# A state-space recurrence in blocks of four steps, inside a five-layer model on one core

## Chip, cores and metric

The kernel runs on one core of a Trainium2 chip. The metric is device microseconds of that core for one execution; every time below is in us unless ns is said.

## What is computed

The model is one hybrid layer, then four others. Only the first layer's state-space branch is touched here. In the reference, `u` has 512 tokens and 512 channels, in 32 groups of 16; each group has 64 complex states:

```python
lb_re = mag * jnp.cos(a_im * dt); lb_im = mag * jnp.sin(a_im * dt)     # lambda, per group and state
bu = einsum('blgc,gpc->blgp', u, bb)                                   # complex input, bb = B (lambda-1)/a
x[t] = lambda * x[t-1] + bu[t]                                         # associative scan over 512 tokens
y = einsum('gcp,blgp->blgc', c_re, x_re) - einsum('gcp,blgp->blgc', c_im, x_im) + d * u
out = gelu(y) * sigmoid(gelu(y) @ w_glu + b_glu)
```

Beside it the same layer has eight attention heads with a difference of two softmaxes, whose q, k and v come from `w_in`, and gates, from `w_in` too.

## The kernel before

Features lie on partitions and the 512 tokens along the free dimension. Dense products are done in three one-pass matmuls on split operands (fp32r, `mm3` and `tok`: lines 251 to 255 and 290 to 292); everything else on TensorE is plain fp32, which each matmul of the program sends as two instructions. A tile framework puts the instructions of all engines in order from a timeline of its own, starting from program order; `weave` interleaves generators step by step in program order.

The recurrence works on 16 tiles of 128 states (two groups each); quarter q holds four tiles j and the 128 channels `u[q]`. A complex scan is made real by rotation: with C and S the cosine and sine of theta*t, the input is turned back by theta*t, scanned with the real factor |lambda| on each lane, and turned forward again. For one tile, `SSM.run` does:

- `tables` (lines 1028 to 1043): C and S for 512 tokens, doubled from 32 in four levels. Each level is two scalings on ScalarE (1040, 1041) and one sum on GpSimd (1042), for C and for S.
- line 1057: two matmuls of the block-diagonal `bb` (32 rows, 128 columns) with `u[q]`, 512 tokens each, into two banks.
- line 1060: four products with C and S from the banks on VectorE; 1061 and 1062: their sum and difference on GpSimd.
- line 1065: two scans over 512 tokens on VectorE.
- line 1067: four products, three on VectorE and one on GpSimd; 1068 and 1069: difference and sum on GpSimd.
- line 1071: two matmuls with the output matrices `cm` (128 rows, 32 columns) into 32 partitions of the bank `y`.

After four tiles line 1075 adds d*u and writes `u[q]` in place. `tab` and `work` have two sets, so that two tiles can be under way.

`first_block` weaves, for p = 0, 1, 2: the two attention heads of pair p (`diff_head`, 8 steps: scores L874 and mask L875, maximum L876, exponential L877, scaling L881, L882, transposes L885, product with v L889), 4, 6 and 6 steps of the recurrence (four steps for each quarter), the projections of pair p + 1 (`pair`: L290 to L292, rotation on VectorE L817, L826 and on GpSimd L823, transposes L833) and 6, 2, 2 of the 16 gate tiles. For p = 3 the two heads go beside `glu`, `sigmoids` and the last six gates. `glu` and `sigmoids` take their scratch from the ring `hf`, which the recurrence uses as well.

Of the kernel before, what the change touches and what calls it, by code (L numbers as in the profile page):

```python
# [16 lines left out]
P = 128  # L17
T = 512
# [21 lines left out]
# ---------------------------------------------------------------- constants of the shapes  # L40
def const_arrays():
# [11 lines left out]
    cols["half"] = ((p[:, None] // 16) % 2 == np.arange(P)[None, :] // 64)  # L53
# [22 lines left out]
class Ring:  # L76
    """tiles that are kept and taken in turn; a use ends, in program order, before the tile's turn comes again"""
# [10 lines left out]
class Kern:  # L88
# [56 lines left out]

    def masks(self):
        """0 and -1e30 above or below the diagonal, and the identity that adds them to a bank"""
# [109 lines left out]
    def wblock(self, w, kts, c0, ncol=256, tok=False, eng=None):  # L257
        """the K chunks of one group of columns: (first k, number of k, tiles)"""
# [6 lines left out]
    def feat(self, blk, j, xh, xl, parts=FULL):  # L265
        """one tile of 128 output features by 512 tokens: [(bank, first token, tokens)]"""
# [13 lines left out]
    def tok(self, blk, xh, xl):  # L280
        """256 output features, tokens on partitions: two banks of [128, 2, 256], one after the other"""
# [13 lines left out]
    def feat_steps(self, blk, j, xh, xl, use):  # L295
        """feat in steps of two k; use(bank) at the end"""
# [10 lines left out]
    def tok_steps(self, blk, xh, xl, use):  # L307
        """tok in steps of four k; use(half, bank) at the end of each half"""
# [28 lines left out]
    def stat(self, i, v, q, part):  # L337
        """sums of v and of its square; the last tile goes straight to the tensor engine"""
# [36 lines left out]
    def rsqrt2(self, v, out=None, log=False, o=0):  # L375
        """-2/sqrt(v): the table's value and one Newton step"""
# [13 lines left out]
    def ln_scale(self, o, w, X, pool=POOLK):  # L390
        """X <- -2 * (X - mean) * rstd, tokens o..; the differences fill the waits of the scale's chain"""
# [33 lines left out]
    def ln_apply(self, gx, bx, gh, bh, parts=HALF):  # L425
        """X <- LN(X)*gx+bx ; H <- LN(X)*gh+bh (columns; the gains carry -1/2)"""
# [31 lines left out]
    def rms_apply(self, g, parts=HALF, log=False):  # L458
        """H <- RMSnorm(X) * g (columns; the gain carries -1/2)"""
# [11 lines left out]
    # ---- feature-major x from and to DRAM  # L471
# [10 lines left out]
    def load_x(self, src, between=None):  # L482
        """x by halves of the tokens, with the mean squares; between: what to load between the halves"""
# [39 lines left out]
    def finish(self, dst, g, b):  # L523
        """the last norm with tokens on partitions: the function that takes 512 features of a tile of tokens"""
# [37 lines left out]
    # ---- adaLN: six vectors of 1024 as columns [128, 48]  # L562
# [11 lines left out]
    def adaln(self, w, brow):  # L574
        """steps of 512 of the 6144 outputs, then the dict of columns in self.mod"""
# [26 lines left out]
    def ln_cols(self, g, b, sc, sh):  # L602
        """columns of x (scaled by alpha for the coming residual) and of h = x*sc + sh"""
# [13 lines left out]
    def add_res(self, n, parts, gate):  # L617
        """X += gate * bank"""
# [8 lines left out]
    def feats(self, tiles, xh, xl, use, halves):  # L627
        """tiles: (block, index) each; use(i, part) takes the bank; by halves of the tokens, all tiles of the first first"""
# [4 lines left out]
    def down4(self, tiles, xh, xl, gate):  # L633
        """tiles 4 to 7 by halves of the tokens: the norm of the first half overlaps the second half"""
# [8 lines left out]
    def logexp(self, a, b):  # L643
        """the table set that has both exp and ln, loaded after a and b are there"""
# [5 lines left out]
    def table(self, func, dep):  # L650
        """have a function's table loaded before it is needed"""
# [96 lines left out]
    def proj_res(self, w, xh, xl, gate, mean=True, early=False):  # L748
        """X += gate * (w^T x), with the sums for the norm; early: the first tiles by halves too"""
# [16 lines left out]
def weave(*gens):  # L766
    """steps of several sequences in turn: (sequence, its number of steps)"""
# [33 lines left out]
def qk_heads(K, blk, tabs, name, out):  # L801
    """two heads of q or k: project, norm, rotate, transpose -> per head [128 = 2 x 64, tokens]"""
# [37 lines left out]
def lam_cols(K):  # L840
    """lambda and the columns [128, 2] it needs"""
# [15 lines left out]
def diff_head(K, q, k, v, nlam, gcol, inv, dst):  # L857
    """q, k: [2 x 64, tokens]; v: [128, 4, 128] by tokens"""
# [47 lines left out]
class SSM:  # L906
    """32 groups of 64 complex states and 16 channels; 16 tiles of 128 states (two groups)"""

    def __init__(self, K, are, aim):
# [14 lines left out]
        mag = self.mag = new("mag")  # L924
# [20 lines left out]
        tr = K.slot("trig")[:, 0:432].rearrange("p (a w i) -> p a w i", a=3, i=16)  # L945
        self.cw, self.sw, self.nsw = tr[:, 0], tr[:, 1], tr[:, 2]
# [4 lines left out]
        nc.gpsimd.tensor_scalar(out=self.nsw, in0=self.sw, scalar1=-1.0, scalar2=None, op0=ALU.mult)  # L951
        # (lambda - 1) / a
        nr, ni, den, x, cr, ci = (new(m) for m in ("nr", "ni", "den", "x", "cr", "ci"))
        tt(nr, mag, self.cw[:, 0, :], ALU.mult)
        nc.gpsimd.tensor_scalar(out=nr, in0=nr, scalar1=-1.0, scalar2=None, op0=ALU.add)
        tt(ni, mag, self.sw[:, 0, :], ALU.mult)
# [12 lines left out]
        # input matrices, block-diagonal, transposed: per four tiles [(j, g, c), 128 states], both parts  # L969
# [6 lines left out]
        self.bb = []  # L976
        tmp = small()[:, 0:256].rearrange("p (i c) -> p i c", c=16)
        for x0, x1, op in ((b[0], b[1], ALU.subtract), (b[1], b[0], ALU.add)):
            bd = small()
            nc.gpsimd.memset(bd, 0.0)  # L980
            bv = bd.rearrange("p (i g c) -> p i g c", g=2, c=16)
            r = small()[:, 0:256].rearrange("p (i c) -> p i c", c=16)
            tt(r, x0, bc(cr), ALU.mult)
            tt(tmp, x1, bc(ci), ALU.mult)
            for g in range(2):
                s = slice(64 * g, 64 * g + 64)
                tt(bv[s, :, g, :], r[s], tmp[s], op)
            ps = K.psa()
            for q in range(4):
# [1156 lines left out]
```

## Time and profile before

| what | value |
|---|---|
| median of three runs | 3927.3 (3927.06 to 3933.09) |
| profiled execution, span | 3925.7 |
| TensorE busy over the span | 3760.0 (96%) |
| VectorE, ScalarE, GpSimd busy | 2621.5, 2095.3, 1517.8 |
| stretch with the recurrence | 100 to 470 |
| in it: TensorE, VectorE, ScalarE, GpSimd busy | 341.0, 292.4, 205.7, 248.2 of 370 |
| in it: granted TensorE clock | 0.89 |

The profiled execution is one further execution of the same kernel, 1.6 below the median of the runs. Busy time of TensorE counts an instruction until its modelled end, at whatever clock was granted, so a busy engine at a clock below 1.00 does less work than the figure says. The clock has two levels, 1.2 and 2.4 GHz; 0.89 is a mean over a stretch.

### The profile page before, as it was taken

To read this page: it belongs to the slowest core of one execution; us is meant where nothing else is said; L and a number is where in the kernel's file an instruction comes from. 1 tells how busy PE (TensorE), PEld (TensorE's weight loads), DVE (VectorE), ACT (ScalarE), POOL (GpSimd) and SP (SyncE) were. 2 spreads that over 40 slices of the span, in tenths; PEclk is the share of its full clock that TensorE was granted. 3 is DMA by queue.
4 is the path that set the end of the run, shared out by engine and by line. 5 is a ranking of instruction groups with operands and counts; after the bars stand their busy time and mean duration, and the time that the engine had idled before them with its cause. 6 is when DMAs were issued, how large, how long until landed. Compare 5 with 4: busy or idle time off the path is not lost.

```text
span 3925.7 us, 51300 instructions
## 1 busy us (share of the span) xinstructions
PE 3760.0 (96%) x19014; PEld 3058.9 (78%) x19014; DVE 2621.5 (67%) x3881; ACT 2095.3 (53%) x3756; POOL 1517.8 (39%) x1456
## 2 busy tenths in 40 slices
PE   8899999999978999999999999999899999999998
PEld 7665678888858887888888788776778788788887
DVE  5688866665698865677676567457776566676545
ACT  4555664555545654476465446654555445555333
POOL 5567602443474543442354341155735340022000
PEclk9898899999989999999999999999999999999999
DMA  5111144554311454332245435442255431132231
GB/s 149 51 60 54 60 145 132 175 182 153 105 62 46 156 178 166 117 104 76 92 154 185 165 116 161 138 140 78 70 175 182 161 118 61 46 105 78 94 105 67
DMA packets 393431, 458.06 MB, mean 117 GB/s; under 512 B 35571, under 2 KB 307357, under 8 KB 393181
## 3 DMA queue, kind: packets, MB, share of 16 engines
q1 hardware_dynamic: 393181, 454.78, 36.0%
q8 instruction: 150, 2.46, 0.3%
q14 instruction: 100, 0.82, 0.1%
HBM read 421.56 MB, written 33.03 MB: 116 GB/s over the span
## 4 chain that ended last, share of the span: by engine, by line
PE 71%; DVE 14%; POOL 5%; DMA 4%; ACT 4%; issue 2%; SPq 0%; DVEq 0%; POOLq 0%; ACTq 0%
PE bank L251 20%; PE bank L254 20%; PE bank L255 20%; DMA mix<-in_ada_w_dram 3%; DVE cacc L1310 3%; DVE wl L237 2%; POOL mix L585 1%; PE bank L1917 1%; ACT mix L583 1%; PE bank L1925 1%; PE bank L317 1%; PE bank L319 1%; PE bank L318 1%; POOL X L453 1%; PE bank L874 1%
## 5 line engine op out<-in xcount | busy, mean ns | idle before, releaser
L251 PE MATMUL bank<-hh,wh 128*128 128x512 f32 (+1 forms) x2928 | 1102.4, 377 | 12.1 <-ACT hh L244 7.4
L254 PE MATMUL bank<-hh,wl 128*128 128x512 f32 (+1 forms) x2928 | 1095.6, 375 | 3.7 <-DVE wl L237 3.7
L255 PE MATMUL bank<-hl,wh 128*128 128x512 f32 (+1 forms) x2928 | 1088.3, 375 | 3.3 <-DVE hl L247 2.1
L237 DVE TENSOR_TENSOR wl<-raw,wh 128x1024 fp32r<-128x1024 f32 (+2 forms) x524 | 676.9, 1293 | 205.0 <-ACT wh L236 199.9
L585 POOL TENSOR_TENSOR mix<-mix,mix 128x512 f32<-128x512 f32 x336 | 501.4, 1492 | 757.7 <-ACT mix L583 739.5
L236 ACT CAST wh<-raw 128x1024 fp32r<-128x1024 f32 (+1 forms) x550 | 562.3, 1026 | 371.8 <-PE bank L255 316.9
L251 PEld LDWEIGHTS bank<-hh,wh 128*128 128x128 f32 x2928 | 558.6, 191 | 126.3 <-ACT hh L244 11.2
L254 PEld LDWEIGHTS bank<-hh,wl 128*128 128x128 f32 x2928 | 558.2, 191 | 110.3 <-DVE wl L237 5.9
L255 PEld LDWEIGHTS bank<-hl,wh 128*128 128x128 f32 x2928 | 551.2, 190 | 113.3 <-DVE hl L247 3.0
L583 ACT ACTIVATE mix<-mix,cs 128x512 f32<-128x512 f32 x384 | 270.3, 722 | 300.6 <-DMA mix<-in_ada_w_dram 299.7
L667 DVE SCALAR_TENSOR_TENSOR mix<-bank,vl,mix 128x510 f32<-128x510 f32 (+3 forms) x384 | 268.8, 700 | 205.8 <-ACT mix L328 197.3
L254 PE MATMUL bank<-uh,wl 128*128 128x512 f32 (+1 forms) x1008 | 371.0, 368 | 3.6 <-DVE wl L237 3.6
L251 PE MATMUL bank<-uh,wh 128*128 128x512 f32 (+1 forms) x1008 | 370.4, 368 | 0.0
L255 PE MATMUL bank<-ul,wh 128*128 128x512 f32 (+1 forms) x1008 | 369.9, 367 | 0.0
L624 DVE SCALAR_TENSOR_TENSOR X<-bank,M,X 128x512 f32<-128x512 f32 (+1 forms) x192 | 120.5, 634 | 235.3 <-PE bank L255 235.1
L254 PEld LDWEIGHTS bank<-uh,wl 128*128 128x128 f32 x1008 | 189.5, 188 | 39.6 <-DVE wl L237 5.3
L251 PEld LDWEIGHTS bank<-uh,wh 128*128 128x128 f32 x1008 | 189.5, 188 | 34.9
L255 PEld LDWEIGHTS bank<-ul,wh 128*128 128x128 f32 x1008 | 189.5, 188 | 34.1
L328 ACT ACTIVATE mix<-bank,vl 128x512 f32<-128x512 f32 (+1 forms) x192 | 141.0, 735 | 85.9 <-PE bank L255 85.6
L244 ACT CAST uh<-mix 128x512 fp32r<-128x512 f32 x110 | 68.0, 618 | 173.5 <-DVE mix L694 173.3
L247 DVE TENSOR_TENSOR ul<-mix,uh 128x512 fp32r<-128x512 f32 x110 | 96.8, 880 | 75.6 <-ACT uh L244 75.1
L358 POOL TENSOR_TENSOR qs<-qs,sq 128x256 f32<-128x256 f32 (+1 forms) x95 | 116.9, 1232 | 53.5 <-ACT sq L343 52.9
(814 smaller groups left out, 7258.5 us busy)
## 6 DMA issues: line engine op xcount, KB each, us to landing
mix<-in_ada_w_dram SPq DMA_DIRECT2D x384, 256.0 KB
raw<-in_ffn_w_up_dram SPq DMA_DIRECT2D x88, 1024.0 KB
raw<-in_ffn_w_down_dram SPq DMA_DIRECT2D x32, 1024.0 KB
raw<-in_w_in_dram SPq DMA_DIRECT2D x22, 1024.0 KB
raw<-in_w_up_dram SPq DMA_DIRECT2D x22, 1024.0 KB
raw<-in_hg_w_in_dram SPq DMA_DIRECT2D x16, 1024.0 KB
raw<-in_ml_w_up_dram SPq DMA_DIRECT2D x16, 1024.0 KB
raw<-in_cc_w_pw_dram SPq DMA_DIRECT2D x12, 1024.0 KB
```

Of the source, the lines that this page charges most:

```text
L236: nc.scalar.copy(out=h, in_=src)
L237: eng.tensor_tensor(out=l, in0=src, in1=h, op=ALU.subtract)
L251: i = mm(out=out, lhsT=wh, rhs=xh, start=start, stop=False)
L254: mm(out=out, lhsT=wl, rhs=xh, start=False, stop=False)
L255: return mm(out=out, lhsT=wh, rhs=xl, start=False, stop=stop)
L328: self.nc.scalar.activation(out=dst[:, o:o + w], in_=ps, func=func, **kw)
L358: nc.gpsimd.tensor_tensor(out=self.qs[:, c], in0=self.qs[:, c], in1=q[:, c], op=ALU.add)
L583: nc.scalar.activation(out=o, in_=o, func=AF.Copy, scale=self.cs[:, k:k + 1])
L585: nc.gpsimd.tensor_tensor(out=acc, in0=acc, in1=o, op=ALU.add)
L624: self.nc.vector.scalar_tensor_tensor(out=x, in0=ps, scalar=gate[:, n:n + 1], in1=x, op0=ALU.mult, op1=ALU.add)
L667: nc.vector.scalar_tensor_tensor(out=d, in0=ps[:, :n - s], scalar=col(s), in1=d, op0=ALU.mult, op1=ALU.add)
L1310: nc.vector.scalar_tensor_tensor(out=acc[:, d], in0=u[:, r], scalar=col(s), in1=acc[:, d], op0=ALU.mult, op1=ALU.add)
```

## The change

The recurrence steps over blocks of four tokens. With token 4n + k, `ub` is `u[q]` seen as four rows of 128 blocks, each read with a stride of four elements. The state at the end of block n is lambda^4 times that of block n - 1, plus the sum over k of lambda^(3-k) B u; the output of token k of a block is the sum over m of `taps` (C lambda^m B) with the inputs of the same block, plus C lambda^(k+1) times the state before the block. So the scan, the rotations and C and S have 128 positions for a tile, and the four tiles of a quarter stand side by side in one instruction of 512. `rho` holds |lambda|^4 with a zero at the start of each tile.

For each quarter `prepare` makes, on VectorE, C and S (`tables`: two doublings for four tiles), lambda^k B (`bd`) and the conjugated lambda^(k+1) C (`cd`); TensorE transposes `bd` into `bb`. Step two multiplies (four accumulating matmuls of 128 blocks per part and tile), copies on ScalarE and rotates; step three scans, rotates back and makes `taps` on TensorE; step four makes the outputs. Each quarter still has four steps. All these tiles have one set; `work` and `cs` are the six `hf` tiles. The constant `half` and its load go. Elsewhere the diff only drops comments. Removed lines, which stand in the functions printed above, are cut:

```diff
...
+        tr = K.slot("trig")
+        tv = tr[:, 0:288].rearrange("p (a w i) -> p a w i", a=2, i=16)
+        self.cw, self.sw = tv[:, 0], tv[:, 1]
...
+        lam = tr[:, 288:448].rearrange("p (x k i) -> p x k i", x=2, i=16)
+        lr, li = self.lr, self.li = lam[:, 0], lam[:, 1]
+        nc.gpsimd.memset(lr[:, 0, :], 1.0)
+        nc.gpsimd.memset(li[:, 0, :], 0.0)
+        mk = mag
+        for w, k in enumerate((1, 2, 4)):
+            if w:
+                m2 = new(f"mag{k}")
+                tt(m2, mk, mk, ALU.mult)
+                mk = m2
+            tt(lr[:, k, :], mk, self.cw[:, w, :], ALU.mult)
+            tt(li[:, k, :], mk, self.sw[:, w, :], ALU.mult)
+        self.mag4 = mk
...
+        self.B = K.slot("ssmB").rearrange("p (x i c) -> p x i c", x=2, c=16)
+        for x, (x0, x1, op) in enumerate(((b[0], b[1], ALU.subtract), (b[1], b[0], ALU.add))):
+            tt(self.B[:, x], x0, bc(cr), ALU.mult)
             tt(tmp, x1, bc(ci), ALU.mult)
...
+            tt(self.B[:, x], self.B[:, x], tmp, op)
...
+            pv = ps.rearrange("p (i g c) -> p i g c", g=2, c=16)
+            for g in range(2):
+                s = slice(64 * g, 64 * g + 64)
+                nc.scalar.activation(out=self.C[s, x], in_=pv[s, :, g, :], func=AF.Copy, scale=sg)
...
         for lev in range(5):
...
+            self.double(C, S, slice(0, 16), lev, tmp, nc.gpsimd)
+        f = small.t + [K.tmp("vrow"), K.rings["sq"].t[0]]
+        self.work, self.cs, self.rho, self.tmp = f[0:4], f[4:6], f[6], f[7]
+        self.taps, self.bb = f[8], f[9:11]
+        self.bd, self.cd = ([K.slot(n) for _ in range(2)] for n in ("bd", "cd"))
+        self.c0 = K.slot("c0")
+        for t in (*self.bd, *self.cd, self.c0, self.taps, self.rho):
+            nc.gpsimd.memset(t, 0.0)
+    def double(self, C, S, tiles, lev, tmp, eng):
+        tt = lambda o, x, y, op: eng.tensor_tensor(out=o, in0=x, in1=y, op=op)
+        w, n = 2 ** lev, tiles.stop - tiles.start
+        cw, sw = (v[:, lev + 2, tiles].unsqueeze(2).to_broadcast([P, n, w]) for v in (self.cw, self.sw))
+        A, B = C[:, :, 0:w], S[:, :, 0:w]
+        for dst, u0, u1, op in ((C, A, B, ALU.subtract), (S, B, A, ALU.add)):
+            o = dst[:, :, w:2 * w]
+            tt(tmp[:, :, 0:w], u1, sw, ALU.mult)
+            tt(o, u0, cw, ALU.mult)
+            tt(o, o, tmp[:, :, 0:w], op)
+    def tables(self, q):
+        tiles = slice(4 * q, 4 * q + 4)
+        C, S = (x.rearrange("p (j n) -> p j n", n=P) for x in self.cs)
+        for o, x in ((C, self.c32), (S, self.s32)):
+            self.K.nc.scalar.copy(out=o[:, :, 0:32], in_=x[:, tiles, :])
+        tmp = self.tmp[:, 0:256].rearrange("p (j n) -> p j n", n=64)
+        for lev in (5, 6):
+            self.double(C, S, tiles, lev, tmp, self.K.nc.vector)
+    def powers(self, src, q, k0, conj, dst):
+        tt = lambda o, x, y, op: self.K.nc.vector.tensor_tensor(out=o, in0=x, in1=y, op=op)
+        t0, t1 = (self.tmp[:, o:o + 256].rearrange("p (k j c) -> p k j c", k=4, c=16) for o in (0, 256))
+        re, im = (src[:, x, 4 * q:4 * q + 4].unsqueeze(1).to_broadcast([P, 4, 4, 16]) for x in range(2))
+        lr, li = (v[:, k0:k0 + 4, 4 * q:4 * q + 4].unsqueeze(3).to_broadcast([P, 4, 4, 16])
+                  for v in (self.lr, self.li))
+        sub, add = (ALU.add, ALU.subtract) if conj else (ALU.subtract, ALU.add)
+        for d, x0, x1, op in ((dst[0], re, im, sub), (dst[1], im, re, add)):
+            dv = d.rearrange("p (k j g c) -> p k j g c", k=4, g=2, c=16)
+            tt(t0, x0, lr, ALU.mult)
+            tt(t1, x1, li, ALU.mult)
+            for g in range(2):
+                s = slice(64 * g, 64 * g + 64)
+                tt(dv[s, :, :, g, :], t0[s], t1[s], op)
+    def prepare(self, q):
+        K, nc = self.K, self.K.nc
+        self.tables(q)
+        self.powers(self.B, q, 0, False, self.bd)
+        for x in range(2):
+            ps = K.psa()
+            for k in range(4):
+                nc.tensor.transpose(out=ps[:, k * P:(k + 1) * P], in_=self.bd[x][:, k * P:(k + 1) * P], identity=K.ident)
+            nc.scalar.copy(out=self.bb[x], in_=ps)
+        self.powers(self.C, q, 1, True, self.cd)
+        c0 = self.c0[:, 0:256].rearrange("p (x j g c) -> p x j g c", x=2, g=2, c=16)
+        for g in range(2):
+            s = slice(64 * g, 64 * g + 64)
+            nc.gpsimd.tensor_copy(out=c0[s, :, :, g, :], in_=self.C[s, :, 4 * q:4 * q + 4])
+        nc.scalar.copy(out=self.rho.rearrange("p (j n) -> p j n", n=P)[:, :, 1:P],
+                       in_=self.mag4[:, 4 * q:4 * q + 4].unsqueeze(2).to_broadcast([P, 4, P - 1]))
     def run(self, q, u, dcol):
...
         K, nc = self.K, self.K.nc
...
+        v = nc.vector
         mm = nc.tensor.matmul
+        self.prepare(q)
+        yield
+        ub = u[q].rearrange("p (n k) -> p k n", k=4)
+        part = [slice(32 * j, 32 * j + 32) for j in range(4)]
+        t, (C, S) = self.work, self.cs
+        for j, r in enumerate(part):
+            c = slice(j * P, (j + 1) * P)
+            pb = K.psm()
+            for x in range(2):
+                o = pb[:, x * P:(x + 1) * P]
+                for k in range(4):
+                    mm(out=o, lhsT=self.bb[x][r, k * P:(k + 1) * P], rhs=ub[r, 3 - k, :], start=k == 0, stop=k == 3)
+                nc.scalar.copy(out=t[2 * x][:, c], in_=o)
+        for o, x0, x1, op, y in ((t[1], t[0], C, None, None), (t[3], t[2], S, ALU.add, t[1]),
+                                 (t[2], t[2], C, None, None), (t[0], t[0], S, ALU.subtract, t[2])):
+            v.tensor_tensor(out=o, in0=x0, in1=x1, op=ALU.mult)
+            if op is not None:
+                v.tensor_tensor(out=o, in0=y, in1=o, op=op)
+        yield
+        for o, x in ((t[1], t[3]), (t[3], t[0])):
+            v.tensor_tensor_scan(out=o, data0=self.rho, data1=x, initial=0.0, op0=ALU.mult, op1=ALU.add)
+        for o, x0, x1 in ((t[0], C, t[1]), (t[1], S, t[1]), (t[2], C, t[3]), (t[3], S, t[3])):
+            v.tensor_tensor(out=o, in0=x0, in1=x1, op=ALU.mult)
+        v.tensor_tensor(out=t[0], in0=t[0], in1=t[3], op=ALU.subtract)
+        v.tensor_tensor(out=t[2], in0=t[2], in1=t[1], op=ALU.add)
+        ps = K.psa()
+        c0 = self.c0[:, 0:256].rearrange("p (x c) -> p x c", x=2)
+        for j, r in enumerate(part):
+            cd = [x.rearrange("p (k c) -> p k c", c=P)[:, 0:3, r] for x in self.cd]
+            for o, w in ((ps[r, 0:32], [c0[:, x, r] for x in range(2)]),
+                         (ps[r, 32:P].rearrange("p (k c) -> p k c", c=32), cd)):
+                for x in range(2):
+                    mm(out=o, lhsT=self.bd[x][:, r], rhs=w[x], start=x == 0, stop=x == 1, tile_position=(0, 32 * j))
+            nc.scalar.copy(out=self.taps.rearrange("p (k c) -> p k c", c=P)[r, :, r],
+                           in_=ps[r, 0:P].rearrange("p (k c) -> p k c", c=32))
+        yield
         y = K.bank["y"]()
...
+        yv = y.rearrange("p (k n) -> p k n", n=P)
+        for k in range(4):
+            mm(out=yv[:, k:4, :], lhsT=self.taps[:, k * P:(k + 1) * P], rhs=ub[:, 0:4 - k, :], start=k == 0, stop=False)
+        for j, r in enumerate(part):
+            for k in range(4):
+                for x, s in ((0, t[0]), (1, t[2])):
+                    mm(out=yv[r, k, 1:P], lhsT=self.cd[x][:, k * P + 32 * j:k * P + 32 * j + 32],
+                       rhs=s[:, j * P:(j + 1) * P - 1], start=False, stop=x == 1 and k == 3,
+                       tile_position=(0, 32 * j))
+        v.scalar_tensor_tensor(out=ub, in0=ub, scalar=dcol[:, q:q + 1], in1=yv, op0=ALU.mult, op1=ALU.add)
         yield
```

## Rows read from the trace of the kernel before

**Rows 1.** Stretches, all engines: busy us (instructions), granted clock, DMA share.
```profile
100.00:200.00 100.00, 90.27 (x403) 67.15 (x404) 67.21 (x98) 51.01 (x142) 55.06 (x72) 0.85 0.17 56
200.00:240.00 40.00, 40.00 (x221) 28.67 (x221) 23.76 (x37) 20.75 (x54) 17.17 (x24) 1.00 0.25 83
240.00:340.00 100.00, 89.79 (x425) 57.38 (x425) 90.92 (x133) 53.15 (x148) 76.32 (x82) 0.90 0.14 46
340.00:470.00 130.00, 120.96 (x590) 80.31 (x589) 110.52 (x156) 80.74 (x207) 99.63 (x101) 0.88 0.15 46
470.00:560.00 90.00, 89.54 (x383) 65.01 (x383) 57.18 (x101) 64.57 (x134) 6.66 (x8) 0.98 0.41 132
```

**Rows 2.** TensorE's own waits, 100 to 470, the three longest.
```profile
PE bank L874 <- ACT mix L877: 7.6, 3, 3.7
PE bank L833 <- DVE mix L826: 4.7, 4, 3.2
PE bank L885 <- DVE mix L882: 4.4, 3, 3.1
```

**Rows 3.** Groups by line, 0 to 475: busy us, mean ns; then idle before.
```profile
L1042 POOL TENSOR_TENSOR hf<-hf,hf 128x32 f32<-128x32 f32 (+3 forms) x128 | 81.1, 636 | 69.9 <-ACT hf L1040 69.8
...
L1040 ACT ACTIVATE hf<-hf,trig 128x32 f32<-128x32 f32 (+3 forms) x128 | 50.0, 392 | 46.3 <-POOL hf L1042 34.5 <-POOL hf L1034 10.8
...
L1065 DVE TENSOR_TENSOR_SCAN sq<-mag,vrow 128x512 f32<-128x512 f32 x8 | 14.2, 1771 | 2.8 <-POOL vrow L1061 2.8
L1062 POOL TENSOR_TENSOR qs<-qs,m 128x512 f32<-128x512 f32 x8 | 13.0, 1619 | 0.0
...
L1060 DVE TENSOR_TENSOR sw<-bank,hf 128x512 f32<-128x512 f32 x16 | 10.6, 678 | 0.0
...
L1061 POOL TENSOR_TENSOR hf<-hf,vs 128x512 f32<-128x512 f32 x8 | 10.2, 1279 | 7.4 <-DVE vs L1060 7.4
L1065 DVE TENSOR_TENSOR_SCAN sw<-mag,sw 128x512 f32<-128x512 f32 x8 | 9.9, 1242 | 0.0
...
L1067 DVE TENSOR_TENSOR hf<-hf,vs 128x512 f32<-128x512 f32 x8 | 7.8, 974 | 0.0
...
L1067 DVE TENSOR_TENSOR sw<-hf,sw 128x512 f32<-128x512 f32 x8 | 5.4, 680 | 0.0
```

**Rows 4.** Groups by shape, VectorE, whole span: a 256-wide operation.
```profile
L399 DVE TENSOR_TENSOR X<-X,bank 128x256 f32<-128x256 f32 x112 | 40.5, 409 | 20.5 <-ACT m L396 19.6 <-POOL vs L356 0.9
```

**Rows 5.** Timeline of TensorE, 232 to 236: start, us, line, shapes, count.
```profile
232.43 0.48 PE L874 MATMUL bank<-kT,qT 64*128 64x128 f32 x2
232.85 0.33 PE L875 MATMUL bank<-maskr,identr 128*128 128x128 f32 x1
233.10 1.98 PE L1057 MATMUL bank<-u,bb 32*128 32x512 f32 x4
235.01 0.66 PE L885 MATMUL bank<-cst,mix 128*128 128x128 f32 x4
```

**Rows 6.** Timeline of TensorE, 466 to 478.
```profile
466.98 1.05 PE L1071 MATMUL bank<-vrow,cm 128*32 128x512 f32 x2
467.87 1.02 PE L1071 MATMUL bank<-sw,cm 128*32 128x512 f32 x2
...
469.16 1.05 PE L889 MATMUL bank<-head,v 128*128 128x128 f32 x8
469.97 0.47 PE L251 MATMUL bank<-hh,wh 128*128 128x512 f32 x1
```

**Rows 7.** Timeline of TensorE's weight loads, same stretch.
```profile
467.44 0.11 PEld L1071 LDWEIGHTS bank<-sw,cm 128*32 128x32 f32 x1 [0.32 <-issue]
```

**Rows 8.** Timeline of TensorE, 979 to 982: a moving operand of stride four.
```profile
980.05 0.36 PE L594 MATMUL bank<-R,cst 128*32 128x48 f32 x8
980.34 0.50 PE L251 MATMUL bank<-uh,wh 128*128 128x512 f32 x1
```

**Rows 9.** Line 1160, the first step of `sigmoids`: ns, first and last start.
```profile
L1160 ACT ACTIVATE hf<-mix x3: 616/629/630, 444.8 to 463.2; 128x512 f32<-128x512 f32 x3
```

More of the change, by code (lines that the diff above doesn't have):

```diff
@@ L923, in __init__ @@
         new = lambda n: K.col([P, 16], n)
-        mag = self.mag = new("mag")
+        mag = new("mag")
         tt(mag, are, dt, ALU.mult)
@@ L950, in __init__ @@
         nc.gpsimd.tensor_scalar(out=self.cw, in0=self.cw, scalar1=-2.0, scalar2=1.0, op0=ALU.mult, op1=ALU.add)
[L951 to L956, printed above, removed]
+        lam = tr[:, 288:448].rearrange("p (x k i) -> p x k i", x=2, i=16)
[11 more added lines that the diff above has]
+        self.mag4 = mk
+        x = new("x")
+        for o, u0, u1, op in ((lr, lr, li, ALU.subtract), (li, li, lr, ALU.add)):
+            tt(x, u1[:, 2, :], li[:, 1, :], ALU.mult)
+            tt(o[:, 3, :], u0[:, 2, :], lr[:, 1, :], ALU.mult)
+            tt(o[:, 3, :], o[:, 3, :], x, op)
+        nr, den, cr, ci = (new(m) for m in ("nr", "den", "cr", "ci"))
+        ni = li[:, 1, :]
+        nc.gpsimd.tensor_scalar(out=nr, in0=lr[:, 1, :], scalar1=-1.0, scalar2=None, op0=ALU.add)
         tt(den, are, are, ALU.mult)
@@ L975, in __init__ @@
         bc = lambda v: v.unsqueeze(2).to_broadcast([P, 16, 16])
-        self.bb = []
         tmp = small()[:, 0:256].rearrange("p (i c) -> p i c", c=16)
[L978 to L983, printed above, removed]
-            tt(tmp, x1, bc(ci), ALU.mult)
[L985 to L989, printed above, removed]
-                nc.tensor.transpose(out=ps[:, q * P:(q + 1) * P], in_=bd[:, q * P:(q + 1) * P], identity=K.ident)
-            self.bb.append(K.slot("bb"))
-            nc.scalar.copy(out=self.bb[-1], in_=ps)
-        self.cm = []
-        hm = K.cload("half")
-        for nm, sg in (("ssm_c_re", 1.0), ("ssm_c_im", -1.0)):
+        self.B = K.slot("ssmB").rearrange("p (x i c) -> p x i c", x=2, c=16)
+        for x, (x0, x1, op) in enumerate(((b[0], b[1], ALU.subtract), (b[1], b[0], ALU.add))):
+            tt(self.B[:, x], x0, bc(cr), ALU.mult)
+            tt(tmp, x1, bc(ci), ALU.mult)
+            tt(self.B[:, x], self.B[:, x], tmp, op)
+        self.C = K.slot("ssmC").rearrange("p (x i c) -> p x i c", x=2, c=16)
+        for x, (nm, sg) in enumerate((("ssm_c_re", 1.0), ("ssm_c_im", -1.0))):
             rows = small().rearrange("p (q g s) -> p q g s", q=4, g=2)
@@ L999, in __init__ @@
                 nc.sync.dma_start(out=rows[:, :, g, :], in_=a[nm][0].rearrange("(q j) c s -> (j c) q s", q=4))
-            half = hm.rearrange("p (g s) -> p g s", g=2).unsqueeze(1).to_broadcast([P, 4, 2, 64])
-            tt(rows, rows, half, ALU.mult)
             ps = K.psa()
@@ L1005, in __init__ @@
                                     identity=K.ident)
-            t = K.slot("cm")
-            nc.scalar.activation(out=t, in_=ps, func=AF.Copy, scale=sg)
-            self.cm.append(t)
+            pv = ps.rearrange("p (i g c) -> p i g c", g=2, c=16)
+            for g in range(2):
+                s = slice(64 * g, 64 * g + 64)
+                nc.scalar.activation(out=self.C[s, x], in_=pv[s, :, g, :], func=AF.Copy, scale=sg)
         C = self.c32 = K.slot("c32").rearrange("p (i w) -> p i w", w=32)
         S = self.s32 = K.slot("s32").rearrange("p (i w) -> p i w", w=32)
-        f = small.t + [K.tmp("vrow"), K.rings["sq"].t[0]] + [K.slot("sw") for _ in range(2)]
-        self.tab = [[*f[2 * i:2 * i + 2], f[4][:, 256 * i:256 * i + 256]] for i in range(2)]
-        self.work = [f[5:9], f[9:13]]
         nc.gpsimd.memset(C[:, :, 0:1], 1.0)
@@ L1018, in __init__ @@
         for lev in range(5):
-            w = 2 ** lev
-            cw, sw = (v[:, lev, :].unsqueeze(2).to_broadcast([P, 16, w]) for v in (self.cw, self.sw))
-            A, B = C[:, :, 0:w], S[:, :, 0:w]
-            for dst, u0, u1, op in ((C, A, B, ALU.subtract), (S, B, A, ALU.add)):
-                o = dst[:, :, w:2 * w]
-                tt(tmp[:, :, 0:w], u1, sw, ALU.mult)
-                tt(o, u0, cw, ALU.mult)
-                tt(o, o, tmp[:, :, 0:w], op)
-    def tables(self, i):
-        K = self.K
-        g = K.nc.gpsimd
-        C, S, tmp = self.tab[i % 2]
-        g.tensor_copy(out=C[:, 0:32], in_=self.c32[:, i, :])
-        g.tensor_copy(out=S[:, 0:32], in_=self.s32[:, i, :])
-        for lev in range(5, 9):
-            w = 2 ** lev
-            c, s, ns = (v[:, lev, i:i + 1] for v in (self.cw, self.sw, self.nsw))
-            for dst, u0, u1, k in ((C, C, S, ns), (S, S, C, s)):
-                o = dst[:, w:2 * w]
-                K.nc.scalar.activation(out=tmp[:, 0:w], in_=u1[:, 0:w], func=AF.Copy, scale=k)
-                K.nc.scalar.activation(out=o, in_=u0[:, 0:w], func=AF.Copy, scale=c)
-                g.tensor_tensor(out=o, in0=o, in1=tmp[:, 0:w], op=ALU.add)
-        return C, S
```

29 lines of the change are left out of this document (removed).

## Prediction

> **What bounds the kernel now.** The first view is the table of stretches [rows 1]. The recurrence runs from 100 to 470, beside attention, projections and gates; before and after it nothing of the change runs but its set-up. TensorE looks busy there, but at a granted clock of 0.85, 0.90 and 0.88 in three of the four stretches. The clock has two levels, and at 1.2 GHz half of the work is done, so a mean of c loses (1 - c) of a stretch: 15 + 10 + 15.6 = 40.6 us. To this comes time in which TensorE does nothing: 9.7 + 10.2 + 9.0 = 29.0. Together some 70 of 370 us are lost, and some 300 us are TensorE's work at the full clock. (Idle time at the low clock is counted in both, so 70 is rather high.) The stretch 200 to 240 shows that it can be otherwise: clock 1.00, no idle time, with VectorE at 59% (23.8 of 40). From 240 to 470 VectorE is at 88% (201.4 of 230) and TensorE loses 45 us. So the stage is no plain TensorE stage: TensorE carries it where the others keep up, and starves where they don't.
>
> What it starves for is in the second view, its waits [rows 2]: the scores wait for ScalarE's exponentials, the transposes for VectorE's sums. These are short chains of attention and projection in engines that go in order, and the third view [rows 3] shows what stands in those queues: the recurrence. GpSimd's sums for the tables (L1042) take 81 us and wait 70 us for ScalarE, while ScalarE's scalings wait 34.5 us for GpSimd: two engines hand 128 small pieces back and forth.
>
> **What is removed.** From [rows 3]: ScalarE loses L1040, 50 us, and its twin L1041 with as many instructions, so some 100. GpSimd loses L1042 and ten groups of eight of 10.2 to 13.0 us, some 118: about 200 in all. VectorE loses L1060 (64 instructions of 0.68, 43), L1065 (four groups, 14.2 to 9.9, 46) and L1067 (six groups, 7.8 to 5.4, 39): 128.
>
> **What is added off TensorE.** VectorE, per quarter: a 512-wide operation is 0.68 [rows 3], a 256-wide one 0.41 [rows 4], so by their slope a 128-wide one 0.27 (an estimate). Tables: six of 128 and six of 256, 4.1. Powers: sixteen of 256, 6.6. Rotations: twelve of 512, 8.2. Two scans at 1.24, 2.5. The last sum was there before. That is 21.4, or 86 for four: 42 less than before. The same operation of L1067 takes 974 ns in one place and 680 in another; with GpSimd nearly empty I expect the low end, which would take a further 10 to 30 us from VectorE's 292. That leaves VectorE near 65% of the stage, between the two stretches above and nearer to the good one. ScalarE gets 14 small copies and three of 512 a quarter, some 25 us in all, by L1040's 392 ns and the 0.62 of a 512-wide activation [rows 9]. In the set-up GpSimd loses two products with the mask and four half-height sums, and gets seven 512-wide memsets, fourteen tiny products and four wide ones; I take that as nothing, hidden while the projections of the first pair feed TensorE. If it isn't, the recurrence starts some us later, and each of its sixteen steps has 370/16 = 23 us.
>
> **What is added on TensorE**, the term against the change. Per quarter, at the full clock:
>
> - Input products. Before, sixteen instructions of 512 columns; a tile's four take 1.91 (233.10 to 235.01 [rows 5]), which is 4 x 0.43 of streaming and 0.2 to begin: 7.6. After, 64 of 128 columns. Eight of that width take 0.81 back to back [rows 6], 0.10 each, so with 0.2 to begin for each tile 7.3. From the other side: if the weights' load shows each time, two take 0.42 as at 232.43 [rows 5], and it is 13.4.
> - Output products. Before, 0.445 an instruction (0.89 for two [rows 6]), sixteen, 7.1. After, 64 of 127 columns, 0.106 of streaming each and the 0.02 that 0.445 holds above 0.427: 8.1. If the whole load of 0.11 shows [rows 7], 13.8.
> - Direct products with `taps`, new: 1280 columns in pairs of instructions that pass twice, 2.1, with a start 2.3.
> - Making `taps`, new: 32 short instructions, 0.05 and 0.10 each, 2.4; with the load shown 5.2.
> - Eight transposes, 0.8; eight of the set-up go.
>
> Sum: 20.9 after, 14.7 before, so 6.2 a quarter and 25 in all. Bounds: 2.5 a quarter (10) if nothing but streaming counts, 20.8 a quarter (83) if every load shows. The instructions of one tile share rows or columns and come in a burst, as the eight of L889 do, so I take 25.
>
> **A rule against it.** The moving operand of the input and direct products is read with a stride of four elements of four bytes. The only row with such a stride is L594 [rows 8]: eight instructions of 48 columns, done in 0.29, less than the 0.32 that eight times 2 x 48 columns at 2.4 GHz take in a row. So these ran partly side by side (four different column groups), and a slower read can neither be seen nor excluded there. The Trainium skill, SBUF — State Buffer, in its note on cachelines ("Door 1: The DMA port swizzle"), says that SBUF has lines of 16 bytes and that each access which goes to a new line pays. Every element of `ub` would be in a line of its own; the trace here does not decide it. If the streaming of strided operands takes twice as long, the input products cost 64 x 0.107 = 6.8 and the direct ones 2.1 more a quarter, 36 in all.
>
> **The sum.** TensorE's work becomes 300 + 25 = 325. Of the 70 us lost I leave: in 100 to 240, half of 24.7 (the first pairs' chains are still there, ScalarE and GpSimd are freed); in 240 to 470, a quarter of 44.9. That is 23.6. The stage then takes 349, 21 less than 370. One thing is late next: `sigmoids` starts at 444.8 [rows 9], before the recurrence ends, in `hf` tiles that the old tables had given free; after, four of these tiles are read until the last quarter's output products. Part of those 25 us of overlap is then lost to ScalarE, while gates keep TensorE fed; I take 4 us, between 0 and 10. So -17: a span of 3909, and with the 1.6 that lie between the profiled span and the median of the runs, 3910.
>
> **Rivals.**
> 1. *Washed out.* The loss falls only to 45, or TensorE's addition is 45 (between 25 and 83): within 8 us of before, 3920 to 3935. For it: the stretch from 100 to 200 loses 25 us with VectorE at only 67%, so relief of VectorE alone need not help.
> 2. *Strided reads stream at half the rate.* TensorE's work is 361. It is then the bound nearly everywhere; with 25 lost, 386, 16 more than before: 3943. It decides as soon as TensorE's addition passes 46 (the 70 lost less the 24 kept). Against it: a plain fp32 instruction takes 0.43 for 512 columns, two cycles a column at 2.4 GHz, so an element may be needed only every second cycle.
> 3. *Attention's chain stays the limit.* The 70 us stay lost and the new work lies on top: 370 + 25, 3952. For it: single sets of tiles, and on VectorE `prepare` is one run of 28 dependent operations (10.7 us) in which a maximum or a sum can be stuck. Against: a quarter's chain is VectorE's 21.4 and TensorE's 20.9, some 42 us, and the weave gives it 370/4 = 92.
> 4. *All is recovered.* The loss is that of 470 to 560, 2.5%: 325/0.975 = 333, 3890.
>
> **Chances.** My forecast 0.55 (its own range 3898 to 3919), all recovered 0.07, washed out 0.17, strided reads 0.12, chain 0.09. A measurement tells 0.2%, 7.9 us, from no change. Faster: 0.55 + 0.07 less the forecast's slow edge, 0.61; same 0.17; slower 0.22. The range reaches from all recovered to the strided reads, 3888 to 3944.
>
> **What would show it.** GpSimd nearly empty between 100 and 450, and VectorE's recurrence near 86 us, would show the removals right. Right on TensorE: 64 short input instructions at 0.10 each; near 0.2 each means that the stride or the load shows. The stretch 240 to 450 should have a clock near 0.97. Wrong: a clock still below 0.9, with scores waiting for exponentials behind a run of `prepare`; or a full clock, no idle time and no shorter stage, which is TensorE's addition. Wrong too if the saving appears by 470 and is gone by 600, when `glu` starts late.

## Result and the profile after

The changed kernel takes 3960.1 us (3954.6 to 3964.8) beside 3927.2 for the kernel before on the same chip: 1.0084 times as long, interval 1.0069 to 1.0098. The forecast was 3910, with a range to 3944. The profiled execution has a span of 3952.9, 27.2 more than before's 3925.7; it is the fastest of the four runs (3954.6), so some 6 of the 32.9 between the medians are not in this trace.

First the stretches of the changed kernel, with the columns of [rows 1]: busy us of TensorE, its weight loads, VectorE, ScalarE, GpSimd, then granted clock, DMA share and GB/s.

```profile
0.00:100.00 100.00, 73.47 (x475) 64.95 (x476) 51.55 (x114) 43.68 (x90) 53.59 (x121) 0.93 0.49 146
100.00:200.00 100.00, 98.62 (x537) 80.36 (x536) 65.63 (x139) 38.98 (x92) 17.00 (x22) 0.85 0.17 57
200.00:240.00 40.00, 40.00 (x251) 30.53 (x250) 14.36 (x31) 13.49 (x28) 0.00 (x0) 1.00 0.18 64
240.00:340.00 100.00, 98.29 (x551) 76.20 (x549) 59.85 (x123) 37.59 (x95) 8.96 (x10) 0.84 0.17 53
340.00:470.00 130.00, 128.25 (x779) 102.80 (x781) 76.41 (x146) 50.63 (x124) 15.04 (x15) 0.87 0.14 46
```

Then TensorE's longest waits from 100 to 470, as [rows 2] gave them before (us in total, times, longest):

```profile
PE bank L289 <- ACT out L327: 1.7, 1, 1.7
PE bank L873 <- ACT kT L834: 1.4, 1, 1.4
PE bank L1075 <- ACT mix L876: 0.8, 1, 0.8
```

From 100 to 470, GpSimd is busy 41.0 us instead of 248.2, VectorE 216.3 instead of 292.4, and TensorE idles 4.8 us instead of 29.0. The long waits of [rows 2] for exponentials and sums are gone. Yet the granted clock is 0.85, 0.84 and 0.87 where [rows 1] had 0.85, 0.90 and 0.88. Before, a low clock stood beside an idle TensorE. Now it stands beside a busy one.

The timeline of TensorE shows what the new matmuls take (start, duration, line, operand shapes, count). The step to the start of the next row is their time; line 1102 is the input products, 1131 the direct ones, 1135 the output products.

```profile
136.95 2.06 PE L1102 MATMUL bank<-u,vrow 32*128 32x128 f32 x10
138.94 0.91 PE L873 MATMUL bank<-kT,qT 64*128 64x384 f32 x2
...
144.87 2.16 PE L1102 MATMUL bank<-u,sq 32*128 32x128 f32 x8
146.95 1.22 PE L888 MATMUL bank<-head,v 128*128 128x128 f32 x4
...
204.33 2.00 PE L1131 MATMUL bank<-u,m 128*128 128x512 f32 x2
206.15 0.62 PE L832 MATMUL bank<-cst,mix 128*128 128x128 f32 x4
...
296.73 4.71 PE L1131 MATMUL bank<-u,m 128*128 128x512 f32 x8
301.37 1.71 PE L1135 MATMUL bank<-hf,cd 128*32 128x127 f32 x14
...
304.06 4.59 PE L1135 MATMUL bank<-hf,cd 128*32 128x127 f32 x50
308.58 0.66 PE L832 MATMUL bank<-cst,mix 128*128 128x128 f32 x4
```

Ten input products take 1.99, 0.20 each instead of 0.10. Two direct products of 512 columns take 1.82, 0.91 each instead of the 0.43 to 0.445 of [rows 5, 6]; a quarter's eight take 4.64, where the forecast had 2.3. The output products, whose operand is contiguous, take 0.090 (4.52 for 50), a little less than the 0.106 of their streaming. So exactly the two that read `ub` with a stride take twice the time. In fine stretches around the first input products (same columns) the clock falls just behind them:

```profile
134.00:138.00 4.00, 4.00 (x18) 2.65 (x17) 3.05 (x6) 1.86 (x3) 2.02 (x2) 1.00 0.79 258
138.00:142.00 4.00, 4.00 (x17) 2.30 (x16) 1.91 (x3) 0.74 (x4) 0.00 (x0) 0.86 0.34 98
142.00:166.00 24.00, 24.00 (x84) 17.95 (x85) 8.01 (x15) 7.78 (x22) 0.00 (x0) 0.50 0.11 39
166.00:170.00 4.00, 4.00 (x17) 3.44 (x16) 3.93 (x7) 1.64 (x4) 0.00 (x0) 0.73 0.00 0
```

For 24 us TensorE is busy without a gap, and the clock is 0.50, the level of 1.2 GHz. What it did before the fall was input products on 32 rows between scores on 64. The other low stretches between 100 and 470 are not shown here; short idle times stand ahead of some of them.

Where the 27.2 arise is read from lines with the same work in both traces (ns of one; first and last start; the pairs of rows are before, after).

```profile
L833 PE MATMUL bank<-cst,mix x12: 270/272/328, 83.4 to 98.7; 128*128 128x128 f32 x12
L832 PE MATMUL bank<-cst,mix x12: 272/273/445, 87.8 to 107.2; 128*128 128x128 f32 x12
...
L833 PE MATMUL bank<-cst,mix x64: 270/295/477, 73.9 to 440.1; 128*128 128x128 f32 x64
L832 PE MATMUL bank<-cst,mix x64: 270/273/477, 77.5 to 463.2; 128*128 128x128 f32 x64
...
L1244 DVE TENSOR_TENSOR hf<-hf,bank x8: 679/687/687, 574.1 to 605.8; 128x512 f32<-128x512 f32 x8
L1307 DVE TENSOR_TENSOR hf<-hf,bank x8: 680/684/687, 602.9 to 633.0; 128x512 f32<-128x512 f32 x8
```

The last transposes of the first pair start at 98.7 before and 107.2 after: 8.5 of set-up. The last transposes of all (line 833, now 832) start at 440.1 and 463.2: 14.6 more in the stage. The last product with the gates (line 1244, now 1307) starts at 605.8 and 633.0: 4.1 more behind it. Nothing is lost later.

### The profile page after: what moved, and what is told of

The parts are those of the page before. It is cut to its first block, busy times and chain, and to the rows that moved or that the text cites. A ratio compares the mean times of both kernels' runs of the same rounds, so it can differ in the third digit from the quotient of the medians.

```text
span 3952.9 us, 52046 instructions
## 1 busy us (share of the span) xinstructions
PE 3793.9 (96%) x19582; PEld 3115.0 (79%) x19582; DVE 2551.3 (65%) x3905; ACT 2040.5 (52%) x3568; POOL 1315.4 (33%) x1238
## 4 chain that ended last, share of the span: by engine, by line
PE 75%; DVE 11%; POOL 4%; DMA 3%; ACT 3%; issue 2%; SPq 0%; DVEq 0%; POOLq 0%; ACTq 0%
PE bank L250 20%; PE bank L253 20%; PE bank L254 20%; DVE cacc L1373 3%; DMA mix<-in_ada_w_dram 3%; DVE wl L236 2%; PE bank L1102 1%; POOL mix L584 1%; PE bank L873 1%; PE bank L1980 1%; PE bank L289 1%; PE bank L290 1%; PE bank L291 1%; POOL X L452 1%; PE bank L1988 1%
```

## Experiments

Ratios are to the kernel before in the same series; its median was 3925.5, 3924.5 and 3926.7 in the three. "The changed kernel" has 1.0084.

**One cause at a time.** Two candidates stand on the same instructions, the stride and the 32 rows. The first experiment copies `u[q]` into block order on GpSimd, once a quarter, and lets both kinds of product read the copy:

```diff
+        nc.gpsimd.tensor_copy(out=self.tmp.rearrange("p (k n) -> p k n", n=P), in_=ub)
...
-    rhs=ub[r, 3 - k, :]
+    rhs=uc[r, 3 - k, :]
...
-    rhs=ub[:, 0:4 - k, :]
+    rhs=uc[:, 0:4 - k, :]
```

> The changed kernel with one copy more per quarter: GpSimd writes the quarter's inputs in block order, side by side, and the input and direct products read that copy, so that no moving operand has a stride. Theory A (strided operands stream at half the rate): an input product falls from 0.20 to 0.11 us an instruction (256 of them, 24 us) and the direct products from 0.91 to 0.45 for 512 columns (8 us), so about 32 us less, some 3928; the clock still falls to its lower level after the input products, if that has another cause. Theory B (the clock, not the stride): each price stays, 3960. If the stride is also what makes the clock fall, its loss of some 45 us goes as well and the kernel is near 3885.

The second keeps the stride and lets the input products use all 128 rows (so each sums the inputs of four tiles and not of its own):

```diff
-    lhsT=self.bb[x][r, k * P:(k + 1) * P], rhs=ub[r, 3 - k, :]
+    lhsT=self.bb[x][:, k * P:(k + 1) * P], rhs=ub[:, 3 - k, :]
```

> The changed kernel with the input products over all 128 rows in place of the 32 of their tile (the sums then hold all four tiles' inputs); instructions, columns and strides stay. Theory B (TensorE's clock falls because instructions on 32 of 128 rows count for little): the granted clock between 100 and 490 rises from about 0.87 to 0.97 or more, the kernel loses some 40 us and comes to about 3920, at 0.20 us an input instruction as before. Theory A alone (the stride costs time, and the clock falls for want of streaming): the clock falls as before, 3960.

The third does both (and computes what the second does).

> The changed kernel with both edits: inputs copied in block order, and input products over all 128 rows (their sums then hold all four tiles' inputs). If stride and rows are two causes that add, 32 us from the first and 40 from the second: about 3888, with a clock of 0.97 or more. If one of them causes the whole, this is no faster than the better of the two single edits.

Measured: copy alone 3945.4, 1.0048 (1.0035 to 1.0060); rows alone 3937.1, 1.0026 (1.0015 to 1.0036); both 3906.2, 0.9942 (0.9930 to 0.9954). The copy is worth 0.36%, the rows 0.58%, and both 1.42%, more than their sum. All three came 17 to 18 short of what was expected for two causes (3928, 3920, 3888). The timeline of the first shows why the copy did: input products with the copy, at the full clock and then at the low one.

```profile
138.12 1.15 PE L1104 MATMUL bank<-qs,vrow 32*128 32x128 f32 x10
139.21 0.91 PE L873 MATMUL bank<-kT,qT 64*128 64x384 f32 x2
...
143.59 2.07 PE L1104 MATMUL bank<-qs,sq 32*128 32x128 f32 x8
145.59 1.22 PE L888 MATMUL bank<-head,v 128*128 128x128 f32 x4
```

At the full clock the copy halves the price, to 0.109 (1.09 for ten; 0.199 with the stride), and a quarter's eight direct products take 2.25 (202.92 to 205.17 in that trace) for 4.64. At the low clock eight input products take 2.00, hardly less than the 2.08 with the stride. So at 1.2 GHz the stride is nearly free, and the copy pays only where the clock is high. The other way round, a higher clock alone takes a strided input product only from 0.26 to 0.20: the rows gave the clock back, and 23 us with it, not the 40 expected. Stretches of 100 us, for the changed kernel (its first stood above, with 0.85), the second and the third experiment:

```profile
...
200.00:300.00 100.00, 99.39 (x577) 76.37 (x576) 46.36 (x95) 35.75 (x85) 3.94 (x5) 0.90 0.16 52
300.00:400.00 100.00, 98.91 (x602) 79.07 (x600) 63.97 (x133) 37.49 (x91) 7.53 (x10) 0.86 0.16 51
```

```profile
100.00:200.00 100.00, 98.54 (x576) 82.02 (x577) 67.13 (x145) 42.81 (x102) 16.88 (x26) 0.97 0.20 69
200.00:300.00 100.00, 99.39 (x615) 77.65 (x615) 50.29 (x101) 34.77 (x86) 4.77 (x6) 1.00 0.12 40
300.00:400.00 100.00, 98.13 (x628) 80.59 (x626) 65.80 (x139) 38.52 (x93) 7.60 (x10) 0.98 0.16 53
```

```profile
100.00:200.00 100.00, 98.62 (x630) 82.01 (x630) 67.61 (x141) 44.20 (x107) 18.72 (x26) 0.98 0.21 69
300.00:400.00 100.00, 98.70 (x699) 83.60 (x699) 64.99 (x127) 43.29 (x109) 13.95 (x15) 0.98 0.11 39
```

With 128 rows, and the same busy share of TensorE, the clock is 0.97 to 1.00. In the first experiment, with 32 rows, it stayed at 0.86, 0.91 and 0.85 in the three stretches. The runs bear it out: over the whole execution the four of the changed kernel have 0.966 to 0.969 and the nine of the second experiment 0.978 to 0.981. Both costs are real, and the low clock hides the other. The second edit uses more rows of both operands, the weights' too; which of them counts is not separated.

**The same rows in the kernel before.** Was before's low clock then a matter of rows too, and not of starvation? Here its input products use 128 rows (again each sums four tiles' inputs):

```diff
-    lhsT=self.bb[x][r, q * P:(q + 1) * P], rhs=u[q][r, :]
+    lhsT=self.bb[x][:, q * P:(q + 1) * P], rhs=u[q]
```

> The kernel before the change, with its input products (line 1057) over all 128 rows in place of the 32 of their tile (the sums then hold all four tiles' inputs); nothing else. Theory B (instructions on 32 rows make TensorE's clock fall, in the kernel before too): the granted clock of 100 to 470 rises from 0.89 to 0.95 or more and the kernel is 10 to 25 us faster, some 3908. The prediction's reading (the clock falls where TensorE starves for VectorE, ScalarE and GpSimd): no change, 3927, clock 0.89.

Measured 3932.5, 1.0017 (1.0006 to 1.0027): no gain, rather 0.17% lost. Its stretches, to be laid beside [rows 1]:

```profile
100.00:200.00 100.00, 87.07 (x416) 63.72 (x414) 68.71 (x100) 53.06 (x148) 58.64 (x76) 0.91 0.20 66
...
240.00:340.00 100.00, 88.18 (x445) 58.14 (x443) 90.99 (x133) 55.76 (x153) 75.00 (x83) 0.95 0.13 43
340.00:470.00 130.00, 115.95 (x550) 76.92 (x551) 108.21 (x151) 76.58 (x196) 92.80 (x98) 0.88 0.15 47
```

The clock rises from 0.85 to 0.91 and from 0.90 to 0.95, stays at 0.88 in the last stretch, and TensorE idles more: 38.8 us from 100 to 470 instead of 29.0. Over the whole execution the trace of before has 0.970 and this one 0.974, but fifteen runs of before in this series have 0.968 to 0.975, mean 0.972, and the eleven of this kernel 0.971 to 0.975, mean 0.973. So the rise is not clear of the spread between runs, and the time does not fall. The rows are not shown to matter in the kernel before; it did wait for the other engines.

**Four tiles in turn.** With the copy, the input products of the four tiles go to four banks and take turns, and so do `taps` and output products, so that neighbours use different rows or columns of TensorE:

```diff
-        for j, r in enumerate(part):
-            for k in range(4):
-                for x, s in ((0, t[0]), (1, t[2])):
+        for k in range(4):
+            for x, s in ((0, t[0]), (1, t[2])):
+                for j, r in enumerate(part):
```

> The changed kernel with the inputs copied in block order, and with the four tiles of a quarter in turn in the input products (four row groups, four banks), the products for the taps and the output products (four column groups), in place of one tile after the other. If row groups and column groups run side by side, an input instruction falls from 0.20 to 0.05 us or less and an output one from 0.09 to 0.04, some 45 us of TensorE at the full clock, and the clock stays up because all rows are in use: about 3880. If they don't run side by side it is e1 again: about 3928.

Measured 3883.9, 0.9882 (0.9867 to 0.9897). The output products on its timeline:

```profile
343.13 1.94 PE L1140 MATMUL bank<-hf,cd 128*32 128x127 f32 x62
345.00 0.44 PE L884 MATMUL bank<-cst,mix 128*128 128x128 f32 x2
```

62 take 1.87, 0.030 each instead of 0.090. Sixteen input products take 0.86 (143.07 to 143.93), 0.054 each. The clock in the three stretches of 100 us is 0.98, 0.87 and 0.93, though the input products still have 32 rows. The time is what was expected with row groups and column groups side by side (3880). The edit changes three kinds of product and the clock at once; what each gave is not separated.

**Stacked inputs.** Sixteen more small GpSimd copies a quarter put the four inputs of a tile's blocks one above the other on 128 rows, so that one matmul over 128 rows does what four accumulating ones over 32 did; the output products take turns as above:

```diff
-                for k in range(4):
-                    mm(out=o, lhsT=self.bb[x][r, k * P:(k + 1) * P], rhs=uc[r, 3 - k, :], start=k == 0, stop=k == 3)
+                mm(out=o, lhsT=self.bb[x][:, c], rhs=t[1][:, c], start=True, stop=True)
```

> The changed kernel with inputs copied in block order, output products and taps with the four column groups in turn (as in e4), and the four inputs of a block stacked on the rows: 16 copies of 32 partitions a quarter on GpSimd, and then one matmul over 128 rows per tile and part in place of four over 32 rows that accumulate (64 instructions in all, not 256). If rows are what the clock falls for: clock 0.97 or more from 100 to 470, and input products of 7 us in place of the 23 of e4, together some 25 us below e4, about 3858. If the clock of e4 falls for another reason, only the 16 us of the products: about 3868. If the copies on GpSimd hold up the rotation of the projections, less than that.

Measured 3875.4, 0.9870 (0.9856 to 0.9885). That is not clear of the fourth experiment's 0.9882, and of the three outcomes named beforehand it is the last: the copies hold up the rotation (line 822) of a pair's projections. In its trace the operand of one rotation leaves VectorE at 256.6 (line 816), but GpSimd gets to it at 266.0:

```profile
254.55 11.38 POOL L1085 COPY hf<-u 32x128 f32<-32x128 f32 x16 [20.50 <-DVE st L385]
266.01 1.98 POOL L822 TENSOR_TENSOR mix<-mix,ABq 128x256 f32<-128x256 f32 x2
```

TensorE idles 17.4 us from 100 to 470 (7.9 in the fourth experiment), and the clock of the three stretches is 0.97, 0.91 and 0.95. From 260 to 270, with TensorE busy 5.8 of 10 us, it is 0.59. So rows are not the only thing before which it falls; idle time is another, as in the kernel before.

**The set-up.** First theory: the seven zero fills on GpSimd delay the first pair. They go to VectorE, in the changed kernel and in the one with stacked inputs (`nc.gpsimd.memset` becomes `nc.vector.memset`).

> The changed kernel with the seven zero fills of the set-up on VectorE in place of GpSimd. Theory C (the set-up's additional work on GpSimd holds up the rotation of the first pair's projections, and TensorE idles some 8 us before 110): 4 to 8 us less, some 3954, and TensorE's busy time in the first 100 us rises from 73 towards the 82 of before. If those waits have another cause: 3960 as before.

> e7 with the seven zero fills of the set-up on VectorE. Theory C: 4 to 8 us below e7. Otherwise the same as e7.

Measured 3959.5, 1.0089 (1.0073 to 1.0104), and 3888.4, 0.9899 (0.9884 to 0.9914), no faster than without the move (the intervals overlap). The theory falls: the last transposes of the first pair start even later, at 112.1 instead of 107.2 and at 113.9 instead of 110.7. The queue of SP in the changed kernel shows something else (line 491 loads x, line 1004 the output matrices C), and TensorE's first transposes of the second half of x wait for it:

```profile
14.86 0.97 SPq L1004 DMA_DIRECT2D vs<-in_ssm_c_re_dram  x2
15.88 0.51 SPq L1004 DMA_DIRECT2D qs<-in_ssm_c_im_dram  x1
17.61 1.83 SPq L491 DMA_DIRECT2D xt<-in_x_dram  x4
```

```profile
21.21 1.00 PE L500 MATMUL bank<-cst,xt 128*128 128x128 f32 x4 [4.93 <-DMA xt<-in_x_dram]
```

Before, the loads of C went out at 55.7 and 61.0, the second half of x at 15.41, and these transposes started at 18.91. The old code loads C into `hf` tiles, the new one into `vs` and `qs`; that these come free earlier is read from the starts of the loads. By GpSimd's first product of the set-up the delay has grown to 6.7 (48.63 to 55.33). The last two experiments keep the loads of C behind those issued ahead of them:

```diff
-                nc.sync.dma_start(out=rows[:, :, g, :], in_=...)
+                K.order(nc.sync.dma_start(out=rows[:, :, g, :], in_=...))
```

> The changed kernel with one thing moved: the four loads of the output matrices C (line 1004) are kept behind the loads that the program issues before them. In the changed kernel SP issues them at 14.86 to 19.48, between the two halves of the loads of x, in the kernel before at 55.73 and 60.96; the second half of x is then late on TensorE (first transpose at 21.21 instead of 18.91), and the first value of the recurrence's set-up on GpSimd comes at 55.33 instead of 48.63. Theory D, the set-up's loss is this place in SP's queue: that value comes at 48 to 50 again, the fourth transposes of the first pair near 100 instead of 106.85, and the time falls by 5 to 9, to about 3952. Rival E, the set-up's loss is given back before the recurrence anyway, or made by GpSimd's own queue after 55: the early marks return but the fourth transposes stay after 104, and the time stays within 3 of 3960.

> The kernel with the four inputs of a block stacked on 128 rows and the output products of four tiles in turn (3875.4), with the four loads of C kept behind the loads that the program issues before them. Theory D: the same 5 to 9 less, about 3868, since TensorE is now less of a bound and a late start counts in full. Rival E: within 3 of 3875.

Measured: in the changed kernel 3956.1, 1.0073 (1.0059 to 1.0086), which its own 1.0084 (1.0069 to 1.0098) overlaps; with stacked inputs 3866.3, 0.9850 (0.9836 to 0.9863), 9 us below 3875.4 (by the ratios 8), the intervals overlapping at the edge. In the first of them GpSimd's product comes at 50.6 and the last transposes of the pair at 103.0, so half of the 8.5 came back by there; with stacked inputs they come at 103.1 instead of 110.7, 7.6 earlier. The loads' place is shown as a cause of the delay; that it costs 8 in the end is not. The last kernel is the fastest of all, 1.5% below the kernel before.

## Why the prediction was wrong

**What bounds the kernel before** was read rightly: it starved, as the run with 128 rows in the kernel before bears out, and the change ended that: 29.0 us of idle time became 4.8.

**The removals** came as forecast on GpSimd (41.0 us left). VectorE's groups by line for the recurrence in the changed kernel, 90 to 480 (busy us and mean ns, then idle before), begin with these:

```profile
L1113 DVE TENSOR_TENSOR hf<-hf,hf 128x512 f32<-128x512 f32 x16 | 14.4, 949 | 0.1
L1106 DVE TENSOR_TENSOR hf<-hf,hf 128x512 f32<-128x512 f32 x16 | 11.0, 690 | 18.4 <-ACT hf L1103 18.3
L1111 DVE TENSOR_TENSOR_SCAN hf<-vs,hf 128x512 f32<-128x512 f32 x8 | 9.7, 1218 | 0.1
```

All of them without the last sum make 91.5, for 86 forecast. The expectation that 974 ns would become 680 with GpSimd nearly empty held. The 949 of line 1113 is a mean that two of its sixteen instructions make; the median is 684. The two stand beside the longest work that GpSimd still has there:

```profile
442.36 5.54 DVE L1113 TENSOR_TENSOR hf<-hf,hf 128x512 f32<-128x512 f32 x2
441.58 5.77 POOL L236 TENSOR_TENSOR wl<-raw,wh 128x1024 fp32r<-128x1024 f32 x2 [12.02 <-ACT wh L235]
```

Without their excess the sum is 87. ScalarE's addition by the forecast's own prices is 29 (56 copies of 0.392, 12 of 0.62), not the 25 written; the trace has some 22.

**The failed step is the price of the strided operand in TensorE's addition.** The forecast gave input and direct products the rate of a contiguous read and put the stride, as rival 2, at 0.12. Its own sign for this, near 0.2 for an input instruction, is what came. Per quarter at the full clock the rows give 64 x 0.199 = 12.7 for 7.3, and 4.6 for 2.3; the output products 64 x 0.090 = 5.8 for 8.1, `taps` 2.3 (0.58 for a tile's eight, 182.19 to 182.77) for 2.4. With 0.8 of transposes that is 26.2 instead of 20.9, and against 14.7 before an addition of 46 in all instead of 25: the very point from which rival 2 was to decide. Its argument against, that an element may be needed only every second cycle, is refuted by 0.91 for 512 columns. By the rule of the Trainium skill, SBUF — State Buffer, in its note on cachelines ("Door 1: The DMA port swizzle"), an access that goes to a new line of 16 bytes pays; the trace agrees at the full clock, with 0.91 beside 0.43 to 0.445, and at 1.2 GHz shows next to nothing (2.08 beside 2.00).

**A second step failed with it:** that the lost clock comes back when the others keep up. Where the clock took 40.6 us in three stretches of [rows 1], by the same measure it takes 47.9 after (15 + 16 + 16.9). The forecast treated low clock and idle time as one loss with one cause. Bursts on 32 rows brought the clock down with no idle time; the second experiment shows it, since only their rows differ. The measure itself, (1 - c) of a stretch, is too high where the stride stays: with the clock back, 23 us were gained, and 39 where the copy had been made (3945.4 to 3906.2). Rival 2's stage, 16 more than before, lies near the measured 14.6, but by two errors that cancel: TensorE's addition is 46 and not its 61, and 53 us are lost (47.9 and the 4.8 of idle time) and not its 25. What the profiled execution (3954.6) has beyond its 3943 is the set-up's 8.5 and the 4.1 behind the stage. The section "What would show it" named a low clock with scores waiting for exponentials, and a full clock without gain; what came was a low clock without waits, which it did not have.

**The set-up**, taken as nothing, cost 8.5 by 107. GpSimd's operations were counted; the four loads of C, which change their place in SP's queue, were not. **The late `sigmoids`** were given 4, and 4.1 were lost behind the stage, but that they did it is not shown: they begin at 455.4, 20.8 ahead of the recurrence's last sum at 476.2, where before they began 24.1 ahead of it (444.8 and 468.9). That the numbers agree may be luck.

With the stride and the 32 rows both taken away the kernel measures 3906, beside the forecast of 3910, though with one copy a quarter more. That is partly luck, for the terms don't agree one by one. In that trace the last transposes of the first pair start at 108.3, 9.6 later than before, for nothing forecast; from there to the last product with the gates (583.1, line 1309) it takes 474.8 instead of 507.1, 32.3 less, where the forecast had 17 less.

Open: why four tiles in turn, still on 32 rows, keep a higher clock in part (0.98, 0.87, 0.93), why the 4.2 us that came back by 103 with the loads of C kept behind don't show clearly in the changed kernel's time, and what makes the 4.1 us behind the stage.

## What to carry to other kernels

When a step turns long matmuls into short ones, price each operand as it is read, stride included, and give a disputed rate the bound of the sum, not a side case: here the stride was worth 32 us of TensorE's time at the full clock (5.8 and 2.3 a quarter, by the prices with and without the copy), more than the whole gain that was forecast. Taken away it gave 15 us, and 31 where the clock was high. A low clock is not always a sign of starvation; look whether the engine is idle beside it, and on how many rows it works, before promising it back. A mean of a group can be made by two instructions; look at the median before explaining it. And when tiles are reassigned, list which loads can now start earlier, and what they get in front of.

## What the runs showed of the hardware

- A four-byte operand with a stride of four elements: 0.91 for 512 columns at the full clock, against 0.43 to 0.445; at 1.2 GHz eight of 128 columns take 2.08 against 2.00.
- TensorE busy without a gap from 142 to 166 at a granted clock of 0.50, behind products on 32 rows; with the same products on 128 rows the stretch from 100 to 200 has 0.97 instead of 0.85. The Trainium skill, TensorE: Matmul & The Clock Gate ("Part 1: The HAM clock gate"), lets the clock follow how busy TensorE has lately been; by busy time as the profile counts it, 24.00 of 24.00 at the low level, the trace doesn't agree, and the measurement decides.
- Output products of four tiles in turn, in four groups of 32 columns, 0.030 each; one tile after the other 0.090. The Trainium skill, TensorEngine Tiling (Array Packing) ("Theoretical Speedup"), gives up to four times for such groups; here it was three.
